# Feeding the last four blocks of the down-projection to the seven-product scheme as well

## The chip, the cores and the metric

The kernel runs on one core of a Trainium2 chip. The metric is the device time of one execution in microseconds (us). Before the change it is 2092.22 us, the median of three runs (2092.10 to 2092.37). The engines are TensorE (PE, matmuls; PEld is its weight load), VectorE (DVE), ScalarE (ACT), GpSimd (POOL) and SyncE (SP, which issues most loads).

## What is computed

Two layers of an encoder over 256 tokens of width 2048, in float32. Cut to the part that the change touches, one layer ends with

```python
h2 = rms_norm(x, ln2_g[l])
u = depthwise_conv(h2 @ w_up[l], conv_w[l], conv_b[l])
gate, up = u[..., :D_FF], u[..., D_FF:]        # D_FF = 5632
x = x + (jax.nn.silu(gate) * up) @ w_down[l]   # (256, 5632) @ (5632, 2048)
```

and the next layer begins with `rms_norm(x, ln1_g) @ w_in`. Ahead of this part stand the two attention groups and the output projection; they are not changed.

## The kernel before, in words

**Precision.** A float32 product is made of three float32r products: each operand is split into a high part (ACT, L112) and a low part (DVE, L113), and high x high, low x high and high x low are added in PSUM. So a product of one 128x128 block of activations with 128x512 weights is three matmuls.

**Weights as a stream.** All weights come in quanta of 128x2048 float32 (1 MB), listed in `quanta` in the order of use (L699 to L729). SP loads a quantum (L741) into one of three `raw` buffers. Each quantum is worked off in steps of 1024 weight columns (two steps; three for a quantum of kind "seven"). Four steps before a step is used, `split_w` (L752) makes its `whi` and `wlo`; there are five buffers of each, and the splits have a raised priority. When the last step of a quantum is split, the load of the quantum three further on is issued.

**The middle and the chunks.** The 5632 middle columns are 44 blocks of 128. `q_up` computes a block (64 pairs of matmuls, two quanta), `glu` (L541) does the conv, the SiLU and the product and leaves the middle `gs[f]`, split, in a tile "mid". The down-projection is done in chunks of 8, 8, 8, 8 and 12 blocks (`CHUNKS`). Output columns 0 to 1023 (nb 0 and 1) of 8 blocks are done pairwise: for a pair of blocks, the 2x2 product over (token halves) x (column halves) takes seven products in place of eight. Six are in `q_seven` (L584): three steps of two products, 18 matmuls 128x512 for a pair; the seventh products of four pairs stand together in a quantum of kind plain (`q_plain`, L639), 12 matmuls, in PSUM tile "mm". `split_seven` (L743) combines the weights on DVE (L747 to L749) ahead of the second step; `sums_mid` (L570) makes the sums and differences of the middles and splits them (L574 to L577 and L580). The six accumulators of a chunk's pairs, `cur["seven"]`, hold one double bank "mm" (of two), both banks "S", and "tr" and "pv": all but one double bank of PSUM. After the chunk's last pair `add_seven` (L611 to L625) adds them to the residual `x`.

Output columns 1024 to 2047 (nb 2 and 3) go through `q_down` (L657): a quantum is four blocks by 512 columns, 24 matmuls in a double bank "mm".

**The last chunk** has 12 blocks. Its first eight go through the plain quantum and four pairs, with the last three `up` blocks between the pairs. Then come, in the order written out at L728, eight quanta of `q_down`: nb 2 for all 12 blocks (three quanta), nb 0 for the last four blocks, nb 3 and nb 1 mixed. The nb 0 and nb 1 quanta accumulate in "mm" and in "tr" and "pv". The last quantum of layer 2 accumulates in the two "S" banks (L679).

**The seam between the layers.** When a column group of `x` is complete, `leave_x` (L627) registers work at a later step: in layer 1 the squares (`square_x`, ACT L140) and the transposes for the next layer (`turn_x`, PE L149, into "S"), whose results `prep_x` splits into the tiles xs0 to xs15 (ACT L115, DVE L116); in layer 2 the output stores. The next layer's first w_in quanta need xs0 to xs3, then xs4 to xs7, and so on.

**What sets the order.** Within an engine the instructions run in an order that is fixed when the kernel is built: by the order of the program, in which work inside `tc.high_priority(offset=...)` counts as that much earlier, and by when buffers come free. So an instruction may be placed behind work that the program lists later. Splits and `add_seven` have an offset of 40 instructions; `add_x` of nb 2, and the plain quantum's add to `x` (L654), have none.

**Tiles for the middles.** `middle` (L518) hands out 17 tiles "mid"; in the last chunk it takes further ones from attention tiles that are idle then (`SPARE`: three "qT").

Of the kernel before, what the change touches and what calls it, by code (L numbers as in the profile page):

```python
# [18 lines left out]
P = 128  # L19
L = 2  # L20
# [32 lines left out]
UP_AT = 56  # L53
WARM = 14

SPARE = 3 * (("qT", 3),)


@with_exitstack
def encoder_kernel(  # L60
# [71 lines left out]
        split(xs[k][:, 0], xs[k][:, 1], src, ln_g[:, which, l, k:k + 1])  # L132

    def square_x(nb):
        if nb == 0:

            st["ss"] = act.tile([P, TT, NB + 24], F32, name="ss_x")[:, :, 0:NB]
        for tt in range(TT):
            sq = work.tile([P, TT, T], F32, name="prob", bufs=2)
            nc.scalar.activation(sq.rearrange("p t n -> p (t n)"), x[:, tt, nb * 512:(nb + 1) * 512], AF.Square,  # L140
                                 accum_out=st["ss"][:, tt, nb:nb + 1])
# [10 lines left out]

    def stat_x(which):
        v = work.tile([P, TT], F32, name="ssum", bufs=2)
        nc.vector.reduce_sum(v, st["ss"], axis=AX.X)
        st["r1"] = act.tile([P, TT], F32, name="r1")
        rsqrt(v, 1.0 / D, st["r1"], "c2")
        if which == 1:

            d = work.tile([P, 4, HD], F32, name="tq", bufs=2)  # L160
            for tt in range(TT):
                nc.vector.tensor_scalar(d[:, tt], ident, st["r1"][:, tt:tt + 1], None, op0=ALU.mult)
            ps = psum.tile([P, T], F32, name="pv", bufs=1)
            mm(ps, ones, d[:, 0:TT].rearrange("p t d -> p (t d)"), True, True)
            st["r2"] = act.tile([P, T], F32, name="acc_b")
            nc.scalar.activation(st["r2"], ps, AF.Copy)
# [351 lines left out]
    def middle(l, f):  # L518

        name, bufs = "mid", MIDS  # L520
        if f >= NF - CHUNKS[-1]:
            k = count[l] = count.get(l, 0) + 1
            if k > MIDS:
                name, bufs = SPARE[k - MIDS - 1]
        return act.tile([P, 2, T], F32R, name=name, bufs=bufs)

    def q_up(l, f, u):
# [13 lines left out]
    def glu(l, f, ps):  # L541
# [20 lines left out]
        gs[f] = middle(l, f)  # L562
        split(gs[f][:, 0], gs[f][:, 1], m)
        ms[f] = m
        if f % 2 and f < NF - CHUNKS[-1] + PART:
            sums_mid(l, f // 2, ms.pop(f - 1), ms.pop(f))

    ms, ss = {}, {}
# [15 lines left out]
    def q_seven(l, c, i):  # L584

        f = sum(CHUNKS[:c]) + 2 * i
        p = f // 2
        a, b = slice(0, P), slice(P, T)

        def body(q, part, hi, lo):  # L590
            if i == 0 and part == 0:
                t = psum.tile([P, 2, 512], F32, name="mm", bufs=2)
                ps = {1: t[:, 0], 6: t[:, 1]}
                for n, name, k in ((5, "S", 2), (7, "S", 2), (3, "tr", 1), (4, "pv", 1)):
                    ps[n] = psum.tile([P, 512], F32, name=name, bufs=k)
                cur["seven"] = ps
            ps = cur["seven"]
            hv, lv = (w.rearrange("p (k n) -> p k n", k=2) for w in (hi, lo))
            todo = (((3, ss[p, 3]), (1, gs[f][:, :, a])),
                    ((7, ss[p, 2]), (5, ss[p, 0])),  # L600
                    ((4, gs[f + 1][:, :, b]), (6, ss[p, 1])))[part]
            for j, (n, x2) in enumerate(todo):
                for x_part, w in ((0, hv), (1, hv), (0, lv)):
                    mm(ps[n], x2[:, x_part], w[:, j], i == 0 and x_part == 0 and w is hv,
                       i == PAIRS - 1 and w is lv)
            if i == PAIRS - 1 and part == 2:
                with tc.high_priority(offset=AHEAD_PRIO):
                    add_seven(ps)
        return body

    def add_seven(ps):  # L611
# [24 lines left out]
            for tt in range(TT):  # L636
                nc.sync.dma_start(out=out[:, tt, m], in_=x[:, tt, m])

    def q_plain(l, c):  # L639

        f0 = sum(CHUNKS[:c])

        def body(q, half, hi, lo):
            if half == 0:
                cur["dn"] = psum.tile([P, TT, 512], F32, name="mm", bufs=2)
            ps = cur["dn"][:, 0]
            hv, lv = (w.rearrange("p (k n) -> p k n", k=2) for w in (hi, lo))
            for x_part, w in ((0, hv), (1, hv), (0, lv)):
                for i in range(2):
                    mm(ps, gs[f0 + 4 * half + 2 * i + 1][:, x_part, 0:P], w[:, i],  # L650
                       half == 0 and i == 0 and x_part == 0 and w is hv, half == 1 and i == 1 and w is lv)
            if half == 1:
                xv = x[:, 0, 0:512]
                nc.vector.tensor_add(xv, xv, ps)  # L654
        return body

    def q_down(l, c, nb, g):  # L657
        f0, nf, i0 = sum(CHUNKS[:c]), CHUNKS[c], FG * g

        def body(q, half, hi, lo):  # L660
            if nb >= 2:
                if nf > PART and i0 == 0 and half == 0:
                    cur["dn"] = psum.tile([P, TT, 512], F32, name="mm", bufs=2)
                ps = cur["dn"]
            elif half == 0:

                ps = cur["dn", nb] = (psum.tile([P, TT, 512], F32, name="mm", bufs=2) if nb == 0 else
                                      _Both(*(psum.tile([P, 512], F32, name=n, bufs=1) for n in ("tr", "pv"))))
            else:
                ps = cur["dn", nb]  # L670
            hv, lv = (w.rearrange("p (k n) -> p k n", k=2) for w in (hi, lo))
            i = i0 + 2 * half

            last = l == L - 1 and c == len(CHUNKS) - 1 and nb == NB - 1
            cut = nf - FG if last or nb < 2 else 0
            if last and i >= cut:
                if i == cut:
                    add_x(nb, ps)
# [14 lines left out]
            with tc.high_priority(offset=4 * AHEAD_PRIO if c == len(CHUNKS) - 1 and nb == NB - 1 else 0):  # L693
                add_x(nb, ps)
            if c == len(CHUNKS) - 1:
                leave_x(q, l, nb, ((3, 0), (1, 1), (5, 0), (1, 1))[nb])
        return body

    for l in range(L):  # L699
# [8 lines left out]
        for c, nf in enumerate(CHUNKS):  # L708
            up = lambda f: [(a["w_up"][l, f, u], q_up(l, f, u), "up") for u in range(2)]
            down = lambda nb, g: [(a["w_down"][l, sum(CHUNKS[:c]) // FG + g, nb], q_down(l, c, nb, g), "")]  # L710
            seven = lambda i: [(a["w_seven"][l, c, i], q_seven(l, c, i), "seven")]

            end = sum(CHUNKS[:c]) + PART + 1
            while f < end:
                quanta += up(f)
                f += 1
            quanta.append((a["w_plain"][l, c], q_plain(l, c), ""))
            if nf == PART:
                for i in range(PAIRS):
                    quanta += seven(i) + down(2 + i // 2, i % 2)  # L720
            else:

                for i in range(PAIRS):
                    quanta += seven(i)
                    if f < NF:
                        quanta += up(f)
                        f += 1
                for nb, g in ((2, 0), (2, 1), (2, 2), (0, 2), (3, 0), (1, 2), (3, 1), (3, 2)):  # L728
                    quanta += down(nb, g)  # L729


    steps = [(q, h) for q in range(len(quanta)) for h in range(3 if quanta[q][2] == "seven" else 2)]
    raw, hl, left, loads, highs = {}, {}, {}, {}, {}

    def load(q, parts=1):
        if q < len(quanta):
            raw[q] = wp.tile([P, 2048], F32, name="raw", bufs=3)
            left[q] = 3 if quanta[q][2] == "seven" else 2
            m = 2048 // parts
            for j in range(parts):  # L740
                loads[q] = nc.sync.dma_start(out=raw[q][:, j * m:(j + 1) * m], in_=quanta[q][0][:, j * m:(j + 1) * m])  # L741

# [138 lines left out]
def _layout(inputs):  # L881
# [29 lines left out]
    o["w_up"] = c(f["w_up"].reshape(L, 2, 8, P, 2, NF, P).transpose(0, 5, 1, 3, 2, 4, 6)).reshape(  # L911
        L, NF, 2, P, 2048)
    wd = f["w_down"]
    n = NF // PART

    four = wd[:, :n * PART * P, :1024].reshape(L, n, PART // 2, 2, P, 2, 512)
    o["w_seven"] = c(np.stack([four[:, :, :, k, :, m] for k, m in ((1, 0), (1, 1), (0, 1), (0, 0))], 4)).reshape(
        L, n, PART // 2, P, 2048)
    o["w_plain"] = c(four[:, :, :, 1, :, 0].transpose(0, 1, 3, 2, 4)).reshape(L, n, P, 2048)
    o["w_down"] = c(f["w_down"].reshape(L, NF // FG, FG, P, NB, 512).transpose(0, 1, 4, 3, 2, 5)).reshape(  # L920
        L, NF // FG, NB, P, 2048)

# [38 lines left out]
```

## Time and profile before

| | |
|---|---|
| median of three runs | 2092.22 us (2092.10 to 2092.37) |
| the profiled execution | 2092.0 us, span 2090.2 us |
| busy: PE, PEld, DVE, ACT, POOL | 2083.5, 1789.2, 1720.5, 1222.3, 170.3 us |
| granted clock of PE | 1.00 |
| DMA | 408.42 MB, mean 195 GB/s |

The profile is of one execution. Its span goes from the first to the last instruction; the 1.8 us between it and the execution's time lie around it. Matmul records overlap (each lasts longer than the distance to the next), so the distance between matmuls is read from groups. The chain of waits is followed back from the last instruction; an engine that isn't on it can be idle without cost.

### The profile page before, as it was taken

How to read it: one execution, taken by the hardware profiler on the slowest of the kernel's cores; microseconds unless marked ns; L12 is line 12 of the kernel's file. 1: busy time of each engine (PE TensorE's matmuls, PEld its weight loads, DVE VectorE, ACT ScalarE, POOL GpSimd, SP SyncE). 2: the span in 40 equal slices, each digit the busy share in tenths (PEclk: the TensorE clock that was granted, in tenths of full speed). 3: DMA queues.
4: the chain of work that ended last, by engine and by line, in shares of the span. 5: the costliest groups of instructions: out<-in, count | busy, mean ns of one | idle time of the engine just before them, and what ended most of it. 6: DMA issues, size and time to landing. Idle time of an engine off the chain costs nothing.

```text
span 2090.2 us, 29185 instructions
## 1 busy us (share of the span) xinstructions
PE 2083.5 (100%) x10816; PEld 1789.2 (86%) x10816; DVE 1720.5 (82%) x2604; ACT 1222.3 (58%) x1817; POOL 170.3 (8%) x237
## 2 busy tenths in 40 slices
PE   9999999999999999999999999999999999999999
PEld 8888888888888888888888888888888888888887
DVE  7786757898898988989757866678989989899896
ACT  7566556555555556556555665565556555555563
POOL 0011100100101001010000011001001010010100
PEclk9999999999999999999999999999999999999999
DMA  9544555556565564655655444555555655556554
GB/s 350 199 145 164 179 172 174 198 195 211 180 241 182 208 210 167 242 193 211 208 181 181 162 160 166 177 182 189 214 202 170 236 199 204 201 185 234 185 200 161
DMA packets 62144, 408.42 MB, mean 195 GB/s; under 512 B 7344, under 2 KB 9904, under 8 KB 13744
## 3 DMA queue, kind: packets, MB, share of 16 engines
q1 hardware_dynamic: 61280, 405.46, 56.2%
q8 instruction: 85, 1.39, 0.3%
q10 hardware_dynamic: 720, 1.08, 0.2%
q14 instruction: 59, 0.48, 0.1%
HBM read 404.42 MB, written 2.10 MB: 194 GB/s over the span
## 4 chain that ended last, share of the span: by engine, by line
PE 99%; DMA 0%; ACT 0%; DVE 0%; issue 0%
PE mm L98 90%; PE S L98 4%; PE pv L98 3%; PE tr L98 2%; PE tr L373 1%; PE tr L307 1%; PE S L149 1%; DMA head<-in_head 0%; ACT qtok L274 0%; ACT kT L315 0%; ACT xs L115 0%; DVE x L688 0%; ACT whi L112 0%
## 5 line engine op out<-in xcount | busy, mean ns | idle before, releaser
L112 ACT ACTIVATE whi<-raw 128x1024 fp32r<-128x1024 f32 (+1 forms) x797 | 830.9, 1057 | 689.9 <-PE mm L98 411.9
L113 DVE TENSOR_TENSOR wlo<-raw,whi 128x1024 fp32r<-128x1024 f32 (+1 forms) x797 | 963.9, 1220 | 270.3 <-ACT whi L112 231.8
L98 PE MATMUL mm<-xs,whi 128*128 128x512 f32 x2816 | 977.0, 390 | 0.0
L98 PE MATMUL mm<-xs,wlo 128*128 128x256 f32 x2816 | 794.1, 282 | 0.0
L98 PEld LDWEIGHTS mm<-xs,whi 128*128 128x128 f32 x2816 | 528.3, 188 | 110.5
L98 PEld LDWEIGHTS mm<-xs,wlo 128*128 128x128 f32 x2816 | 532.2, 189 | 1.1
L98 PE MATMUL mm<-whi,mid 128*128 128x512 f32 x1412 | 368.2, 391 | 0.0
L98 PEld LDWEIGHTS mm<-whi,mid 128*128 128x128 f32 x1412 | 263.0, 188 | 53.9
L98 PE MATMUL mm<-whi,xs 128*128 128x512 f32 x1152 | 294.2, 393 | 1.4 <-ACT qtok L274 1.3
L98 PEld LDWEIGHTS mm<-whi,xs 128*128 128x128 f32 x1152 | 213.1, 188 | 44.7 <-ACT qtok L274 1.8
L98 PE MATMUL mm<-wlo,mid 128*128 128x512 f32 x706 | 202.4, 392 | 0.0
L98 PE MATMUL mm<-wlo,xs 128*128 128x512 f32 x576 | 159.5, 393 | 0.0
L98 PEld LDWEIGHTS mm<-wlo,mid 128*128 128x128 f32 x706 | 132.1, 188 | 27.0
L557 DVE SCALAR_TENSOR_TENSOR pT<-halo,conv,pT 128x256 f32<-128x256 f32 x352 | 148.1, 478 | 0.9
L549 POOL COPY halo<-halo 128x6 f32<-128x6 f32 x88 | 39.6, 450 | 1232.6 <-DVE halo L547 1232.6
L98 PEld LDWEIGHTS mm<-wlo,xs 128*128 128x128 f32 x576 | 107.3, 188 | 21.6
L555 ACT ACTIVATE pT<-halo,conv 128x256 f32<-128x256 f32 x176 | 95.1, 587 | 5.8 <-DVE halo L547 5.7
L550 POOL COPY halo<-halo 128x6 f32<-128x6 f32 x88 | 77.1, 876 | 0.2 <-POOL halo L549 0.2
L547 DVE TENSOR_TENSOR halo<-prob,acc_b 128x512 f32<-128x512 f32 x88 | 60.6, 689 | 1.9
L546 DVE TENSOR_TENSOR prob<-prob,mm 128x512 f32<-128x512 f32 x88 | 59.8, 679 | 0.0
L545 ACT ACTIVATE prob<-mm 128x512 f32<-128x512 f32 x88 | 51.3, 583 | 7.1 <-PE mm L98 7.1
L559 ACT ACTIVATE prob<-pT 128x256 f32<-128x256 f32 x88 | 35.5, 404 | 30.0 <-DVE pT L557 30.0
(180 smaller groups left out, 1475.4 us busy)
## 6 DMA issues: line engine op xcount, KB each, us to landing
raw<-in_w_up SPq DMA_DIRECT2D x176, 1024.0 KB, 4.9
raw<-in_w_in SPq DMA_DIRECT2D x71, 1024.0 KB, 4.9
raw<-in_w_down SPq DMA_DIRECT2D x48, 1024.0 KB, 4.8
raw<-in_w_seven SPq DMA_DIRECT2D x40, 1024.0 KB, 4.9
raw<-in_w_out SPq DMA_DIRECT2D x32, 1024.0 KB, 4.9
raw<-in_w_plain SPq DMA_DIRECT2D x10, 1024.0 KB, 4.8
bias<-in_bias SPq DMA_DIRECT2D x16, 160.0 KB, 3.1
x<-in_x SPq DMA_DIRECT2D x4, 512.0 KB, 10.7
```

Source lines behind the costliest of these rows:

```text
L98: nc.tensor.matmul(ps, lhsT, rhs, start=start, stop=stop, skip_group_check=True)
L112: high = nc.scalar.activation(hi, src, AF.Copy)
L113: nc.vector.tensor_sub(lo, src, hi.bitcast(F32))
L149: nc.tensor.transpose(ps[:, j, tt * P:(tt + 1) * P], x[:, tt, (k + j) * P:(k + j + 1) * P], ident)
L545: nc.scalar.activation(t, ps[:, :, 0], AF.Copy)
L546: nc.vector.tensor_add(t, t, ps[:, :, 1])
L547: nc.vector.tensor_mul(ux[:, :, r:r + T], t, st["r2"][:, None, :].to_broadcast([P, 2, T]))
L549: nc.gpsimd.tensor_copy(ux[:, :, 1:r], ux[:, :, T:T + r - 1])
L550: nc.gpsimd.tensor_copy(ux[:, :, T + r:T + 2 * r - 1], ux[:, :, r + 1:2 * r])
L555: nc.scalar.activation(y[:, j, :], ux[:, j, r:r + T], AF.Identity, scale=w1, bias=b)
L557: nc.vector.scalar_tensor_tensor(y[:, j, :], ux[:, j, o:o + T], w, y[:, j, :], op0=ALU.mult, op1=ALU.add)
L559: nc.scalar.activation(t[:, 0, :], y[:, 0, :], AF.Silu)
```

## The change

The last chunk's four remaining blocks (40 to 43) go through the pair scheme too, for output columns 0 to 1023. Two pairs, and half a quantum of plain products (kind "half": one step, half the load), take the place of the four blocks' nb 0 and nb 1 quanta. The pairs' accumulators stay open until the sixth pair. The order at the chunk's end becomes: nb 2 (three quanta), pair 5, the half plain, pair 6, nb 3 (three quanta). The middles' sums need four more tiles per layer, taken from "kT", "kTb" and "v_a". nb 0 and nb 1 leave (squares and transposes, or stores) after `add_seven`, registered two and three quanta after pair 6; nb 2 is registered two quanta after its last one, at the half plain. The weights on the host are laid out accordingly: w_seven with 22 pairs per layer, w_plain with 6 quanta, the last one half filled. The sums are the same in exact arithmetic.

```diff
-SPARE = 3 * (("qT", 3),)
+STEPS = {"seven": 3, "half": 1}
+
+SPARE = 3 * (("qT", 3),) + 2 * (("kT", 2),) + (("kTb", 1), ("v_a", 1))
...
     def square_x(nb):
-        if nb == 0:
+        if "ss" not in st:
...
-        nc.vector.reduce_sum(v, st["ss"], axis=AX.X)
+        nc.vector.reduce_sum(v, st.pop("ss"), axis=AX.X)
...
+        if name == "v_a":
+            return act.tile([P, 2, 2, T], F32R, name=name, bufs=bufs)[:, 0]
         return act.tile([P, 2, T], F32R, name=name, bufs=bufs)
...
-        if f % 2 and f < NF - CHUNKS[-1] + PART:
+        if f % 2:
             sums_mid(l, f // 2, ms.pop(f - 1), ms.pop(f))
...
+            pairs = CHUNKS[c] // 2
...
-                       i == PAIRS - 1 and w is lv)
-            if i == PAIRS - 1 and part == 2:
+                       i == pairs - 1 and w is lv)
+            if i == pairs - 1 and part == 2:
                 with tc.high_priority(offset=AHEAD_PRIO):
                     add_seven(ps)
+                if c == len(CHUNKS) - 1:
+                    for nb in range(2):
+                        leave_x(q, l, nb, ((2, 0), (3, 0))[nb])
...
-    def q_plain(l, c):
+    def q_plain(l, c, g=0):
-        f0 = sum(CHUNKS[:c])
+        f0 = sum(CHUNKS[:c]) + PART * g
+        steps = CHUNKS[c] // 4
         def body(q, half, hi, lo):
-            if half == 0:
+            first, last = half == 0, half == 1 or 2 * g + half == steps - 1
+            if first:
                 cur["dn"] = psum.tile([P, TT, 512], F32, name="mm", bufs=2)
...
-            if half == 1:
+            if last:
                 xv = x[:, 0, 0:512]
                 nc.vector.tensor_add(xv, xv, ps)
...
-                leave_x(q, l, nb, ((3, 0), (1, 1), (5, 0), (1, 1))[nb])
+                leave_x(q, l, nb, ((2, 0), (1, 1))[nb - 2])
...
-                for nb, g in ((2, 0), (2, 1), (2, 2), (0, 2), (3, 0), (1, 2), (3, 1), (3, 2)):
-                    quanta += down(nb, g)
+                quanta += down(2, 0) + down(2, 1) + down(2, 2) + seven(4) + plain(1) + seven(5)
+                quanta += down(3, 0) + down(3, 1) + down(3, 2)
-    steps = [(q, h) for q in range(len(quanta)) for h in range(3 if quanta[q][2] == "seven" else 2)]
+    steps = [(q, h) for q in range(len(quanta)) for h in range(STEPS.get(quanta[q][2], 2))]
...
-            m = 2048 // parts
+            m = (1024 if quanta[q][2] == "half" else 2048) // parts
```

## Rows read from the trace of the kernel before

**Rows 1.** the page's busy times: us, share of the span, instructions of each engine.

```profile
PE 2083.5 (100%) x10816; PEld 1789.2 (86%) x10816; DVE 1720.5 (82%) x2604; ACT 1222.3 (58%) x1817; POOL 170.3 (8%) x237
```

**Rows 2.** the page's chain that ended last, by engine.

```profile
PE 99%; DMA 0%; ACT 0%; DVE 0%; issue 0%
```

**Rows 3.** the chain in time, layer 2's last chunk: start, us, what.

```profile
1996.96 11.33 PE mm L98 x65
...
2042.54 21.99 PE mm L98 x97
...
2068.61 5.44 PE mm L98 x24
```

**Rows 4.** PE in time, first and last matmuls of that chunk.

```profile
1990.22 1.08 PE L98 MATMUL mm<-whi,mid 128*128 128x512 f32 x4
...
2085.67 0.61 PE L98 MATMUL S<-wlo,qT 128*128 128x512 f32 x2
```

**Rows 5.** the chain in order of time at the seam of the layers.

```profile
1034.21 2.72 PE mm L98 x12
1036.93 0.88 PE S L149 x8
1037.81 9.08 PE mm L98 x40
```

**Rows 6.** busy time by engine in stretches: us, then busy us, PE's clock, DMA.

```profile
572.67:582.01 9.34, 9.34 (x43) 7.75 (x42) 9.23 (x10) 5.46 (x7) 0.00 (x0) 1.00 0.54 195
...
1001.00:1018.00 17.00, 17.00 (x77) 14.08 (x76) 16.91 (x23) 9.36 (x13) 2.19 (x2) 1.00 0.76 265
1018.00:1045.00 27.00, 27.00 (x125) 22.46 (x124) 17.37 (x19) 15.05 (x26) 0.00 (x0) 1.00 0.57 195
1045.00:1066.00 21.00, 21.00 (x106) 17.50 (x105) 13.21 (x19) 12.61 (x22) 0.70 (x1) 1.00 0.51 168
...
2059.00:2087.00 28.00, 27.29 (x121) 22.27 (x119) 13.77 (x14) 5.87 (x6) 0.00 (x0) 1.00 0.27 100
```

**Rows 7.** DVE's groups from 1990 to 2040: busy us, mean ns, idle before.

```profile
L747 DVE TENSOR_TENSOR raw<-raw 128x1024 f32<-128x1024 f32 x3 | 3.6, 1215 | 0.0
L749 DVE TENSOR_TENSOR raw<-raw 128x512 f32<-128x512 f32 x4 | 2.7, 684 | 0.0
...
L113 DVE TENSOR_TENSOR mid<-tq,mid 128x256 fp32r<-128x256 f32 x2 | 0.8, 415 | 0.0
L654 DVE TENSOR_TENSOR x<-x,mm 128x512 f32<-128x512 f32 x1 | 0.7, 675 | 0.0
...
L577 DVE TENSOR_TENSOR tq<-bias,tq 128x128 f32<-128x128 f32 x1 | 0.3, 280 | 0.0
```

**Rows 8.** the page's group of ACT's high parts: busy us, mean ns, idle before.

```profile
L112 ACT ACTIVATE whi<-raw 128x1024 fp32r<-128x1024 f32 (+1 forms) x797 | 830.9, 1057 | 689.9 <-PE mm L98 411.9
```

**Rows 9.** DMA issues: count, KB each, median us to landing.

```profile
raw<-in_w_down SPq DMA_DIRECT2D x48, 1024.0 KB, 4.8
raw<-in_w_seven SPq DMA_DIRECT2D x40, 1024.0 KB, 4.9
```

**Rows 10.** DVE in time, a middle chunk and layer 2's end.

```profile
574.75 4.62 DVE L113 TENSOR_TENSOR wlo<-raw,whi 128x1024 fp32r<-128x1024 f32 x4
...
583.20 1.22 DVE L481 TENSOR_TENSOR x<-x,mm 128x1024 f32<-128x1024 f32 x1
...
2042.81 0.69 DVE L617 TENSOR_TENSOR x<-x,mm 128x512 f32<-128x512 f32 x1
...
2054.01 1.21 DVE L622 TENSOR_TENSOR x<-x,S 128x1024 f32<-128x1024 f32 x1
...
2058.88 0.68 DVE L625 TENSOR_TENSOR x<-x,pv 128x512 f32<-128x512 f32 x1
```

**Rows 11.** DVE in order of time at the seam, the first four preps.

```profile
1039.07 0.87 DVE L116 SCALAR_TENSOR_TENSOR xs<-S,head,xs 128x256 fp32r<-128x256 f32 x2
...
1041.91 0.87 DVE L116 SCALAR_TENSOR_TENSOR xs<-S,head,xs 128x256 fp32r<-128x256 f32 x2
```

More of the change, by code (lines that the diff above doesn't have):

```diff
@@ L650, in body @@
                     mm(ps, gs[f0 + 4 * half + 2 * i + 1][:, x_part, 0:P], w[:, i],
-                       half == 0 and i == 0 and x_part == 0 and w is hv, half == 1 and i == 1 and w is lv)
-            if half == 1:
+                       first and i == 0 and x_part == 0 and w is hv, last and i == 1 and w is lv)
+            if last:
                 xv = x[:, 0, 0:512]
@@ L660, in body @@
         def body(q, half, hi, lo):
[L661 to L670, printed above, removed]
+            if nf > PART and i0 == 0 and half == 0:
+                cur["dn"] = psum.tile([P, TT, 512], F32, name="mm", bufs=2)
+            ps = cur["dn"]
             hv, lv = (w.rearrange("p (k n) -> p k n", k=2) for w in (hi, lo))
@@ L674, in body @@
             last = l == L - 1 and c == len(CHUNKS) - 1 and nb == NB - 1
-            cut = nf - FG if last or nb < 2 else 0
+            cut = nf - FG if last else 0
             if last and i >= cut:
@@ L710, in encoder_kernel @@
             down = lambda nb, g: [(a["w_down"][l, sum(CHUNKS[:c]) // FG + g, nb], q_down(l, c, nb, g), "")]
-            seven = lambda i: [(a["w_seven"][l, c, i], q_seven(l, c, i), "seven")]
             end = sum(CHUNKS[:c]) + PART + 1
@@ L716, in encoder_kernel @@
                 f += 1
-            quanta.append((a["w_plain"][l, c], q_plain(l, c), ""))
+            first = sum(CHUNKS[:c]) // 2
+            seven = lambda i: [(a["w_seven"][l, first + i], q_seven(l, c, i), "seven")]
+            plain = lambda g: [(a["w_plain"][l, c + g], q_plain(l, c, g), "half" if g else "")]
+            quanta += plain(0)
             if nf == PART:
@@ L737, in load @@
             raw[q] = wp.tile([P, 2048], F32, name="raw", bufs=3)
-            left[q] = 3 if quanta[q][2] == "seven" else 2
-            m = 2048 // parts
+            left[q] = STEPS.get(quanta[q][2], 2)
+            m = (1024 if quanta[q][2] == "half" else 2048) // parts
             for j in range(parts):
@@ L913, in _layout @@
     wd = f["w_down"]
[L914 to L919, printed above, removed]
+    n = NF // 2
+    four = wd[..., :1024].reshape(L, n, 2, P, 2, 512)
+    o["w_seven"] = c(np.stack([four[:, :, k, :, m] for k, m in ((1, 0), (1, 1), (0, 1), (0, 0))], 3)).reshape(
+        L, n, P, 2048)
+    plain = np.zeros((L, -(-n // 4) * 4, P, 512), np.float32)
+    plain[:, :n] = four[:, :, 1, :, 0]
+    o["w_plain"] = c(plain.reshape(L, -1, 4, P, 512).transpose(0, 1, 3, 2, 4)).reshape(L, -1, P, 2048)
     o["w_down"] = c(f["w_down"].reshape(L, NF // FG, FG, P, NB, 512).transpose(0, 1, 4, 3, 2, 5)).reshape(
```

## The prediction

> **What bounds the kernel now.** I read the page's busy shares first: PE is busy for 2083.5 of 2090.2 us, DVE for 82%, ACT for 58% [rows 1]. The chain that ended last is 99% PE [rows 2], so nothing but matmul time, and idle time of PE, can move the end. Busy matmul records overlap, so I take the price of a matmul from the chain in order of time: a group of 24 matmuls 128x512 takes 5.44 us, 0.2267 us each [rows 3]. The stretch that the change edits is dense. In layer 2, 97 matmuls from 2042.54 on take 21.99 us, again 0.2267 each, and a block of w_up (64 of the 65 in one piece of 11.33 us) takes 11.1 us [rows 3]. From the last chunk's first plain matmul, at 1990.22, there are 12 + 72 + 192 matmuls 128x512 at 0.2267 us and three blocks of w_up, 95.9 us, which gives 2086.1; the last two matmuls begin at 2085.67 and end by 2086.3 [rows 4]. So no hole is in it. The seam between the layers is as dense: twelve matmuls of a down, eight transposes and the next matmuls follow within 0.05 us [rows 5]. The granted clock is 1.00 (the 2.4 GHz level) in every stretch [rows 6].
>
> DVE is the engine to watch. In the middle of a chunk, where a pair of blocks and a w_down quantum alternate, it is busy for 9.23 of 9.34 us while PE never waits [rows 6]: a full DVE is covered as long as its work is spread over the four steps by which splits run ahead. After the last pair it has room: 17.37 of 27 us and 13.21 of 21 us at the seam, 13.77 of 28 us at the end [rows 6].
>
> **Matmuls.** Per layer the change takes away two w_down quanta (columns 0 to 1023, blocks 40 to 43): 2 x 24 = 48 matmuls. It adds two pairs at 18 and half a plain quantum, 6: 42. That is 6 fewer per layer, 12 in all, 12 x 0.2267 = 2.72 us, and all of it is on the path, because PE is the path. The Trainium skill (TensorE: Matmul & The Clock Gate, section Back-to-back issue gap) gives about 131 ns per matmul of 512 columns as the sustained rate of a real kernel; by that the saving would be 1.57 us, an estimate. The trace doesn't agree: 24 matmuls in 5.44 us are 227 ns each.
>
> **DVE and ACT.** A split of 1024 columns costs DVE 1.16 us in a run (4.62 us for four [rows 10]) and ACT 1.06 [rows 8]. A pair has three splits and, before its second part, three combinations of weights, 1.2 + 0.7 + 0.7 = 2.6 us [rows 7]. The sums of a pair's middles are four operations of 0.28 us and two splits of 0.42, 2.0 us on DVE [rows 7]; on ACT two splits, which I take at the same 0.42. Added per layer on DVE: 7 splits (8.1), two sets of combinations (5.2), two sets of sums (4.0), one plain add (0.7): 18.0 us. Removed: 4 splits (4.6), one add of 1024 columns (1.2) and two of 512 (1.4): 7.2. Net 10.8 us at most, since neighbours overlap. From the end of the fourth pair to the seam's end (1001 to 1066) DVE now works 16.91 + 17.37 + 13.21 = 47.5 of 65 us [rows 6]; with 8.8 more (one set of sums falls earlier) it is 56.3 of 63.6 us. So the total fits, and I cost DVE's and ACT's extra work at nothing where it can spread. ACT gains 7 - 4 = 3 splits and four short ones, about 5 us, and is far from full.
>
> **The tight place.** Let T be the end of the three downs of columns 1024 to 1535 (2042.54 + 16.33 = 2058.9 in layer 2 of the trace). From there PE runs pair 5 (T to T+4.1), the half plain (to T+5.4), pair 6 (to T+9.5) and the first of the three downs of columns 1536 to 2047. There are five buffers for split weights, so the split of pair 6's first part can start at T: ready at T+2.2. Its combinations end at T+4.8, the second part's high half comes at T+5.9 and its low half at T+7.0. PE needs the high half at T+6.8, and the low half four matmuls later, T+7.7. The third part is ready at T+8.2 and its low half is needed at T+9.1; the first half of the next down is ready at T+9.3 and its low half is needed at T+11.3. It holds with 0.7 to 0.9 us to spare: no stall from splits, but the lead is used up here.
>
> **Loads.** Two w_down loads of 1 MB go, two w_seven loads of 1 MB and one of half that come, 0.5 MB more per layer. A 1 MB load lands in 4.8 to 4.9 us [rows 9], and the next down's load goes out when pair 5 is split, about T-2, so it is there at T+3, before its buffers are free. SP carries nothing else here but output stores and, at the seam, two small bias loads. Cost nothing; if that cover went, a late load would cost up to its 4.9 us.
>
> **Waits that the change adds.** The accumulators of the pairs (one double bank "mm", both "S", "tr", "pv") are now held until after pair 6, some 26 us longer. Queued behind that: the additions of the pairs' sums (they were drained between 2042.81 and 2059.56, 16.7 us from the first to the end of the last, sharing DVE with the block's conv and the splits [rows 10]); then, in layer 1, the squares and transposes for the next layer, which need "S"; in layer 2, the last two halves, which accumulate in "S". The sums themselves are 6.5 us of DVE, six of 0.68 and two of 1.2 [rows 7]. After T+9.5 only splits compete (1.16 in each 2.72 us), so they end at about T+9.5 + 6.5/0.57 = T+20.9, and "S" is free at T+18. Layer 2's last quantum needs "S" at T+20.4: enough. At the seam the transposes of columns 1024 to 1535, which come first in the order, take "S" at T+18; four preps took from 1036.93 to 1042.78 [rows 5, 11], 5.9 us, so the transposes of columns 0 to 511 start at T+23.9, and their first prep ends 2.6 us after, as there (1039.07 + 0.48), at T+26.5. w_in's first matmul is due at T+25.9. The lower end is the seam of before, with no wait; the upper end is rival 2. I take the 0.6 us that this gives, once.
>
> **Sum.** The profiled execution took 2092.0 us (span 2090.2); 2092.0 - 2.72 + 0.6 = 2089.9. The median of the runs is 0.2 above it: 2090.1 us.
>
> **Rivals.**
> 1. A bank that isn't free (slower than before). The half plain accumulates in the second "mm" bank; the first belongs to the pairs. The down behind pair 6 needs that bank, so it waits for the plain's add on DVE, due at T+5.4. That add has no raised priority and the splits have. If DVE takes it at once, nothing is lost. If it stands behind the splits of pair 6 and of the next downs (four to six splits, to T+10.5 or T+12.8), the add ends at T+11.2 to T+13.5 and PE stops for 1.7 to 4 us; 2.6 in each layer gives 2092.2 - 2.7 + 5.2 = 2094.7. It decides from 1.36 us per layer on. Against it: adds of this kind got a slot soon after their matmuls (an add of 1024 columns at 583.20, between two splits, on a DVE that was full [rows 10]). For it: DVE has its densest 10 us exactly there. The Trainium skill (PSUM — Partial Sum Buffer, section Engine vs sequencer instructions) says that VectorE's queue is strictly first in, first out; by that, whatever place the compiled order gives the add, nothing passes it. No row here shows it directly. Chance 0.17.
> 2. The seam jams. If the sums take the 16.7 us of now instead of 11.4, the first preps come 5.3 us later and w_in stops for up to 5.5 us, and layer 2's last quantum waits some 1.5 us for "S" (L622 starts 11.2 us after the first sum [rows 10]). Half of that, 3.5 us, gives 2093.0; all of it 2096.5. Against: there is no block's conv beside the sums any more. Chance 0.15.
> 3. Everything is covered, no stall at all: 2089.5. It is the lower end of the forecast's own case.
> 4. A gain beyond the matmuls: there is no idle PE to win in the edited stretches, so I give it 0.03.
>
> **How the numbers follow.** The forecast with its edges (stalls of 0 to 2 us, 2089.4 to 2091.6) has 0.65, rival 1 0.17, rival 2 0.15, rival 4 0.03. The range 2089.2 to 2093.4 holds the first, half of the second rival and the milder third of rival 1 (one layer only, 2092.1), some 8 in 10. A measurement of this kernel tells about 0.2%, 4.2 us, from no change: below 2088.0 or above 2096.4. Faster by that would need 1.5 us more than the matmuls removed: 0.03. Slower by that needs stalls of 6.9 us, rivals 1 and 2 at their upper ends together: 0.06. Within: 0.91.
>
> **What would show it.** Chain still 99% PE; groups of 24 matmuls at 5.44 us; pair 6 beginning 5.44 us after pair 5; no hole before the first down behind pair 6 (if there is one, the DVE add of the plain's bank stands at its end: rival 1); no hole before the first w_in matmul of layer 2 (else rival 2). DVE about 1741 us busy, w_down loads 44, w_seven 44, w_plain 12. I am wrong if the time leaves 2089.2 to 2093.4, or if PE shows holes of over 2 us in all.

## The result, and the profile after

The changed kernel takes 2099.97 us (median of five runs, 2099.66 to 2101.36) against 2092.22 us before it: ratio 1.0039 [1.0029, 1.005]. It is 7.8 us slower, where 2090.1 us was forecast with a range up to 2093.4. The profiled execution took 2099.89 us (span 2098.1). One execution of run 4 below was slow (7316 us) and is left out of that run's median.

The page after: busy times, then the chain that ended last by engine (they answer to [rows 1, 2]).

```profile
PE 2084.9 (99%) x10804; PEld 1788.9 (85%) x10804; DVE 1739.8 (83%) x2642; ACT 1229.6 (59%) x1831; POOL 170.2 (8%) x237
...
PE 98%; DVE 1%; ACT 0%; DMA 0%; issue 0%; DVEq 0%
```

The 12 matmuls are gone (10816 to 10804), and DVE and ACT have the work that was foreseen. Yet PE's share fell and DVE stands in the chain with 1%. So PE now stops. The waits of PE say where (us in total, times, longest); the `qtok` and `halfpi` rows stood there before too, 1.3 and 1.1 us.

```profile
PE S L151 <- DVE xs L118: 4.7, 1, 4.7
PE mm L100 <- ACT qtok L276: 1.3, 2, 0.7
PE mm L100 <- DVE prob L550: 1.1, 2, 0.6
```

To place the loss, follow one landmark through both traces: the first products into "S" of a pair. Of the first pair in layer 1's last chunk they begin at 952.43 before and 952.47 after, so all before that is equal. Of the fourth pair, 998.69 and 999.99 (+1.30). Of layer 2's first pair, 1993.63 and 2001.69 (+8.06). Of its fourth, 2039.89 and 2048.99 (+9.10). So the losses are 1.30 us between the pairs of layer 1, 8.06 - 1.30 + 1.36 = 8.1 us at the seam of the layers (1.36 us is the six matmuls saved in between), and 1.04 us between the pairs of layer 2. 1.30 + 8.1 + 1.04 - 2 x 1.36 = 7.7; the spans differ by 7.9.

**Between the pairs.** PE and DVE in order of time, layer 1, in the last w_up blocks (start, us, engine, line, what, count, wait before it):

```profile
987.42 0.50 PE L100 MATMUL mm<-xs,whi 128*128 128x512 f32 x1 [0.63 <-DVE prob L550]
```

```profile
982.20 0.29 DVE L579 TENSOR_TENSOR tq<-tq,bias 128x128 f32<-128x128 f32 x1
982.40 0.42 DVE L115 TENSOR_TENSOR qT<-bias,qT 128x256 fp32r<-128x256 f32 x1
982.74 1.22 DVE L115 TENSOR_TENSOR wlo<-raw,whi 128x1024 fp32r<-128x1024 f32 x1
983.87 0.28 DVE L581 TENSOR_TENSOR tq<-bias,tq 128x128 f32<-128x128 f32 x1
984.08 1.22 DVE L115 TENSOR_TENSOR wlo<-raw,whi 128x1024 fp32r<-128x1024 f32 x1
985.21 0.42 DVE L115 TENSOR_TENSOR qT<-tq,qT 128x256 fp32r<-128x256 f32 x1
985.55 1.22 DVE L115 TENSOR_TENSOR wlo<-raw,whi 128x1024 fp32r<-128x1024 f32 x1
986.68 0.68 DVE L550 TENSOR_TENSOR prob<-prob,mm 128x512 f32<-128x512 f32 x1
```

DVE has no idle time from 982.20 on. The new sums of the fifth pair (L579, L581 and their splits) stand between weight splits, and L550, the add that frees the "mm" bank for the next w_up block, stands behind all of it. PE waits for that bank. About 0.4 of layer 1's 1.30 us are lost earlier, at 971.55, where the chain of waits goes through late weight splits. DVE had little room here, 47.43 us busy of the 50 from 952 to 1002 before the change; but run 5 will show that the order of its work made these holes, not the amount.

**At the seam.** PE in order of time, then DVE:

```profile
1044.95 1.03 PE L151 MATMUL S<-ident,x 128*128 128x128 f32 x8
1050.66 2.06 PE L151 MATMUL S<-ident,x 128*128 128x128 f32 x8 [4.68 <-DVE xs L118]
1052.61 0.79 PE L100 MATMUL mm<-whi,xs 128*128 128x512 f32 x1
1053.65 2.07 PE L100 MATMUL mm<-whi,xs 128*128 128x512 f32 x4 [0.25 <-ACT xs L117]
```

```profile
1026.26 5.76 DVE L115 TENSOR_TENSOR wlo<-raw,whi 128x1024 fp32r<-128x1024 f32 x5
1031.93 0.68 DVE L625 TENSOR_TENSOR x<-x,mm 128x512 f32<-128x512 f32 x1
1033.56 2.36 DVE L115 TENSOR_TENSOR wlo<-raw,whi 128x1024 fp32r<-128x1024 f32 x2 [0.94 <-ACT whi L114]
1035.84 0.68 DVE L627 TENSOR_TENSOR tq<-tq,mm 128x512 f32<-128x512 f32 x1
1036.71 1.23 DVE L115 TENSOR_TENSOR wlo<-raw,whi 128x1024 fp32r<-128x1024 f32 x1 [0.19 <-ACT whi L114]
...
1044.19 1.22 DVE L632 TENSOR_TENSOR x<-x,tq 128x1024 f32<-128x1024 f32 x1
1045.32 1.21 DVE L483 TENSOR_TENSOR x<-x,mm 128x1024 f32<-128x1024 f32 x1
1046.45 1.22 DVE L115 TENSOR_TENSOR wlo<-raw,whi 128x1024 fp32r<-128x1024 f32 x1
1047.59 0.68 DVE L633 TENSOR_TENSOR x<-x,pv 128x512 f32<-128x512 f32 x1
```

`add_seven`'s sums (L625 to L633) need each other's results and alternate with splits; the last ends at 1048.27. From the start of the first to the end of the last they took 16.3 us, and seven splits stand between them. That is nothing new: before the change the same eight sums took 16.7 us (layer 2, 2042.81 to 2059.56), with seven splits among them as well:

```profile
L113 DVE TENSOR_TENSOR wlo<-raw,whi 128x1024 fp32r<-128x1024 f32 x7 | 8.4, 1218 | 0.0
```

Columns 0 to 511 of `x`, which w_in's first products need, are complete only then. PE has run out of w_down products at 1044.95, turns nb 2 and stops; nb 2's preps (L118), which would free the banks for the next transposes, queue on DVE behind the last sum. From the last sum to the transposes at 1050.66 the chain of waits goes through ScalarE, where the squares of the new `x` (L142) stand ahead of a prep:

```profile
1048.30 1.33 ACT prob L142 x4
1049.64 0.37 ACT xs L117
...
1050.03 0.50 DVE xs L118
```

Before the change the first twelve products of a w_down, eight transposes and the next products followed each other without a gap there [rows 5]. The windows of this stretch, with PE's granted clock as the third number from the end (the layout of [rows 6], where it was 1.00):

```profile
1018.00:1045.00 27.00, 27.00 (x121) 22.32 (x120) 25.38 (x27) 16.32 (x21) 0.00 (x0) 1.00 0.75 273
1045.00:1056.00 11.00, 6.08 (x25) 4.32 (x24) 7.19 (x14) 6.77 (x19) 0.69 (x1) 0.70 0.29 95
```

So of the seam's 8.1 us, 4.92 us is idle PE (11.00 - 6.08). The rest is mainly the lower clock level (granted 0.50 from 1051 to 1055, 1.2 GHz) after the stop: eight transposes take 2.06 us in place of 1.03, four products 2.07 in place of 1.07.

### The profile page after: what moved, and what is told of

Same layout as the page of the kernel before. It is cut to its first block, busy times and chain, and to the rows that moved or that the text cites. A ratio compares the mean times of both kernels' runs of the same rounds, so it can differ in the third digit from the quotient of the medians.

```text
span 2098.1 us, 29235 instructions
## 1 busy us (share of the span) xinstructions
PE 2084.9 (99%) x10804; PEld 1788.9 (85%) x10804; DVE 1739.8 (83%) x2642; ACT 1229.6 (59%) x1831; POOL 170.2 (8%) x237
## 4 chain that ended last, share of the span: by engine, by line
PE 98%; DVE 1%; ACT 0%; DMA 0%; issue 0%; DVEq 0%
PE mm L100 89%; PE S L100 4%; PE pv L100 2%; PE tr L100 1%; PE tr L375 1%; PE tr L309 1%; PE S L151 1%; DVE wlo L115 1%; DMA head<-in_head 0%; DVE prob L550 0%; ACT xs L117 0%; ACT qtok L276 0%; ACT prob L142 0%; ACT prob L549 0%; DVE x L483 0%
## 5 line engine op out<-in xcount | busy, mean ns | idle before, releaser
L550 DVE TENSOR_TENSOR prob<-prob,mm 128x512 f32<-128x512 f32 x88 | 59.9, 681 | 3.4 <-ACT prob L549 3.4
L752 DVE TENSOR_TENSOR raw<-raw 128x1024 f32<-128x1024 f32 x44 | 53.8, 1222 | 0.6
```

Source lines behind the costliest of these rows:

```text
L550: nc.vector.tensor_add(t, t, ps[:, :, 1])
L752: nc.vector.tensor_sub(w[:, 1:3], w[:, 1:3], w[:, 2:4])
```

## The experiments

The theory after reading the traces: the sums at the seam come late because DVE rebuilds the lead of splits that pairs 5 and 6 use up. The rivals: layer 2's part of the change, the order of the transposes, the priority of the sums, the "S" banks, ScalarE's squares. The kernel before ran beside each on the same chip (2092.10 to 2092.28 us).

**1. The change in layer 2 alone** (the old last chunk kept in layer 1).

```diff
...
-            pairs = CHUNKS[c] // 2
+            pairs = CHUNKS[c] // 2 if l == 1 else PAIRS
...
```

> The change in layer 2 alone; layer 1 keeps the old order of its last chunk. My theory (the loss is at the seam of the layers: PE waits 4.7 us for a bank S and then runs some 3 us at the lower clock, about 8 us; beside it each layer loses some 1.1 us in the w_up blocks between the pairs and wins 1.36 us of matmuls): 2092.2 - 1.36 + 1.04 = 2091.9 us, no hole at the seam. Rival (each layer loses alike, half of the 7.7 us): 2096.1 us.

Measured: 2092.58 us, ratio 1.0002 [0.9993, 1.0012]. Without the change at the seam the 7.8 us are gone, which speaks for the theory and against the rival; the saving of 1.36 us does not show. In this trace layer 2's fourth pair begins 0.93 us late, and behind it PE waits another 0.49 us for L550 (to 2044.21): together they use up the saving.

**2. Columns 1024 to 1535 turned last** instead of first.

```diff
-                leave_x(q, l, nb, ((2, 0), (1, 1))[nb - 2])
+                leave_x(q, l, nb, ((6, 1), (1, 1))[nb - 2])
```

> Squares and transposes of columns 1024 to 1535 registered after those of columns 0 to 1023, nothing else; it acts at the seam only. Theory that the order of the S banks makes the hole (columns 1024 to 1535 take both banks first, and w_in's first block waits for their four preps): the hole goes nearly, 2094 us or less. Theory that the sums of the pairs are late (the last addition to columns 0 to 511 ends 3 us after PE has run out of downs, so no order helps before that): the hole shrinks from 8 to about 5 us, 2097 us.

Measured: 2100.87 us, 1.0041 [1.0026, 1.0055]. Both forecasts (2094 or less, 2097) were missed. PE waited in other places, and no shorter, 6.3 us in all (start, us, what, wait; a further wait of 1.76 us for a prep follows):

```profile
1044.45 0.38 PE L151 MATMUL S<-ident,x 128*128 128x128 f32 x2
1047.91 0.88 PE L151 MATMUL S<-ident,x 128*128 128x128 f32 x6 [3.09 <-DVE x L633]
1050.25 0.80 PE L100 MATMUL mm<-whi,xs 128*128 128x512 f32 x1 [1.46 <-ACT xs L117]
```

Two of the eight transposes run, the other six wait for `x` itself, for the last sum (L633). The order of the transposes isn't the cause; the lateness of the sums is enough to stop PE.

**3. A fourfold priority for the sums** (`offset=4 * AHEAD_PRIO` around `add_seven` in the last chunk).

> The additions of the pairs' sums in the last chunk get four times the raised priority, so that they stand ahead of the splits of the next steps. Late-sums theory: they end some 6 us earlier, the seam's hole falls to 0 to 2 us, some 1 us is lost to later splits behind pair 6: 2093 to 2095 us. Order-of-S theory: the transposes of columns 1024 to 1535 still stand at the end of the downs and hold S, so 2098 us or more.

Measured: 2100.17 us, 1.0039. No gain, where the late-sums theory had 2093 to 2095: DVE's order stayed the same, L625 at 1031.61 and L633 at 1047.10. ACT's one step of the sums (L626) stood behind two splits that waited 3.0 us for a w_down load. I read it so (argued, not tested): a priority can't raise a step whose operand isn't there, and in each gap of the chain the next split is ready. Since the order did not change, this run doesn't test what earlier sums would bring.

**4. The sums of the middles registered later** in the last chunk, to clear the w_up stretch.

> The sums of the middles of the last two pairs are registered one pair later, nothing else. Theory that these small DVE operations, put between the splits, upset the order in the w_up blocks (holes of 0.6 us twice per layer): both layers win about 1.1 us back, 2097.7 us with the seam's hole as it is. Rival (the holes come from the split of the weights or the loads there): no change, 2100 us.

Measured: 2100.7 us (four runs), 1.0041. Inconclusive: the built order still took the one operation whose operands are ready early (the difference of the first block's halves) at the same place, at 962.88, and PE's waits for L550's add, one in each layer, stayed (0.8 us).

**5. That operation made late by its data.** v2 = m1a - m1b is also m2b - v1, and v1 needs the pair's second block; the last two pairs of a layer use that.

```diff
-        nc.vector.tensor_sub(v[:, 2], m1[:, a], m1[:, b])
+        if p < NF // 2 - 2:
+            nc.vector.tensor_sub(v[:, 2], m1[:, a], m1[:, b])
+        else:
+            nc.vector.tensor_sub(v[:, 2], m2[:, b], v[:, 1])
```

> For the last two pairs the third of the four middles' differences is computed from the pair's other sum (the same value but for rounding), so that it can't run before the pair's second block is done; nothing else. Theory (that 0.2 us operation, which DVE took between two weight combinations, flips the order of ACT's queue, so that ACT waits for a w_up block before five splits, and PE loses 0.6 us there in each layer): the first hole of each layer goes, 2098.8 us, and the fourth pair of layer 1 starts some 0.6 us earlier. Rival (the other sums or the loads): no change, 2100 us.

Measured: 2098.59 us (2097.30 to 2099.81), 1.0031 [1.0019, 1.0043]. The waits between the pairs are gone in both layers; the fourth pair of layer 1 begins its products into "S" at 998.74 (998.69 before, 999.99 after). In the changed kernel the early difference (L580) stood between two combinations of weights, and ACT then put its step for a w_up block ahead of five splits and waited for it:

```profile
962.97 0.29 DVE L580 TENSOR_TENSOR tq<-bias 128x128 f32<-128x128 f32 x1
...
967.17 0.60 ACT L549 ACTIVATE prob<-mm 128x512 f32<-128x512 f32 x1 [2.94 <-PE mm L100]
967.67 4.84 ACT L114 ACTIVATE whi<-raw 128x1024 fp32r<-128x1024 f32 x5
```

In run 5 that order is gone. DVE has as many sums to do and is even busier, 48.30 of the 50 us, and PE is busy for all 50:

```profile
952.00:1002.00 50.00, 50.00 (x267) 43.28 (x266) 48.30 (x66) 32.01 (x43) 3.53 (x6) 1.00 0.60 209
```

So the order made the holes between the pairs, and not the amount of work. The stop at the seam remains:

```profile
1049.17 0.63 PE L151 MATMUL S<-ident,x 128*128 128x128 f32 x4 [4.51 <-DVE xs L118]
```

**6 to 8. Pairs 5 and 6 earlier**, so that more w_down products lie behind them: right after the first nb 2 quantum (early_pairs), one quantum later (spread_pairs), and the first of these with the tied sum (early_pairs_tied).

```diff
...
-                quanta += down(2, 0) + down(2, 1) + down(2, 2) + seven(4) + plain(1) + seven(5)
-                quanta += down(3, 0) + down(3, 1) + down(3, 2)
+                quanta += (down(2, 0) + seven(4) + down(2, 1) + seven(5) + down(2, 2) + down(3, 0) + plain(1)
+                           + down(3, 1) + down(3, 2))
```

(These are the lines of early_pairs; spread_pairs puts each pair one quantum later.)

> The same work in another order: pair 5 after the first down of columns 1024 to 1535, pair 6 after the second, the half plain after the first down of columns 1536 to 2047 (in its own bank), columns 0 to 1023 leaving after it. Pair 6 ends 6.8 us earlier and has 5.4 us of other matmuls between it and pair 5. Late-sums theory: the sums end before the last down, the seam's hole of 8 us goes, and 2092.2 - 2.7 + 2.3 (the holes in the w_up blocks stay) = 2091.8 us. Rival (DVE has too much to do in the last chunk, whatever the order): 2096 us or more.

> As the run above, but each pair one down later: pair 6 ends only 1.4 us earlier than in the changed kernel, while 5.4 us of other matmuls lie between the pairs. Theory that the sums are late because pair 6 ends late: the hole at the seam stays at about 5 us, 2097 us. Theory that the sums are late because the two pairs stand side by side and use up the lead of the splits: the hole goes, 2092 us.

> The early order with the tied difference. If both theories hold: 2092.2 - 2.7 + 1.0 = 2090.5 us, faster than both kernels; if the tied difference does nothing, as early_pairs.

Measured: 2099.55 (1.0038), 2098.46 (1.0029) and 2097.94 us (1.0026 [1.0016, 1.0037]). All three missed their theory's time (2091.8, 2092 and 2090.5); only part of the loss came back. In early_pairs the sums end at 1043.5 and not at 1048.3, and yet PE stops: 1.8 us for the bank of the sums (L627, both layers) and 2.2 us for nb 0's preps.

```profile
PE mm L100 <- ACT xs L117: 2.2, 1, 2.2
PE mm L100 <- DVE tq L627: 1.8, 2, 0.9
```

So an earlier end of the sums alone isn't enough; the preps, squares and nb 3's add queue on DVE and ACT behind them.

spread_pairs tested whether the sums are late because the two pairs stand side by side and use up the lead of the splits. It speaks against that: its time is nearer to the other theory's 2097. The sums took 16.5 us from first to last there and 18.5 in early_pairs, against 16.3 in the changed kernel. Moving the pairs does not shorten the chain of sums. In spread_pairs the chain of waits at the seam goes back to a w_down load (1025.45 to 1031.15).

**9. Layer 2 alone, with the tied sum.**

> The new scheme in layer 2 alone (layer 1's last chunk as before the change), and the one sum of the last two pairs that was ready early made out of the pair's late results. Theory of the holes between the w_up blocks: layer2_only measured 2092.58 with the second layer's hole of 1.04 us still in it; that hole goes, the six matmuls fewer stay: 2091.2 to 2091.6, no PE wait in layer 2's last chunk. Rival (the small op's place did not make layer 2's hole, the tied sum helped in layer 1 alone): 2092.6 as layer2_only.

Measured: 2091.31 us (2090.79 to 2092.11, 11 runs), 0.9995 [0.9986, 1.0004], no wait of PE in layer 2's last chunk. The expectation holds: the holes of run 1 (0.93 and 0.49 us) are gone, and the six matmuls of this layer are won in the trace, whose span is 1.2 us below that of before. It is 0.97 us below the kernel before in the medians, which the interval doesn't yet tell from none.

**10. "S" read early.** With the tied sum, products 5 and 7 leave their "S" banks as soon as pair 6's second step is done: `read_s` adds product 5 to `x` and copies product 7 into SBUF on ACT.

```diff
...
+            if c == len(CHUNKS) - 1 and i == pairs - 1 and part == 1:
+                with tc.high_priority(offset=AHEAD_PRIO):
+                    read_s(ps)
...
```

> tied_sum, and in the last chunk products 5 and 7 are read out of the two S banks as soon as pair 6's second part is done (one add, one extra ACT copy), so that nb 2's transposes need not wait for add_seven's later sums. Theory of the late sums: nb 0's x is still finished by the last sum some 13 to 15 us after pair 6's last part, so nb 2 is turned early but the first w_in products, which need nb 0, still start late: stop of 3 to 5 us at the layer seam and the low clock after it, 2096.5 to 2098.5. Rival (the S banks are what holds the seam): the stop goes, with it the low clock: 2098.6 - 4.5 - 0.6 - 2.4 = 2091.1.

Measured: 2098.24 us, 1.0028 [1.0017, 1.0039]. As the late sums have it: nb 2 is turned at 1033.67, 10 us earlier, and nothing is gained, since w_in begins with nb 0:

```profile
1046.67 0.88 PE L151 MATMUL S<-ident,x 128*128 128x128 f32 x6 [1.75 <-DVE x L648]
1048.39 0.50 PE L100 MATMUL mm<-whi,xs 128*128 128x512 f32 x1 [0.85 <-ACT xs L117]
1050.95 2.07 PE L100 MATMUL mm<-whi,xs 128*128 128x512 f32 x4 [2.06 <-ACT xs L117]
```

**11. The same, and layer 2's first w_in job begins with nb 2.** Its sum over the input columns is taken in another order.

```diff
...
-            for u in range(4):
-                quanta.append((a["w_in"][l, j, u], q_win(l, j, u), ""))
+            order = (2, 0, 1, 3) if l > 0 and j == 0 else range(4)
+            for n, u in enumerate(order):
+                quanta.append((a["w_in"][l, j, u], q_win(l, j, u, n == 0), ""))
```

> free_s_tied, and the second layer's first w_in job reads its four weight tiles in the order nb 2, nb 0, nb 1, nb 3, so that TensorE has 24 products (24 x 0.2267 = 5.4 us) of nb 2 while the sums of nb 0 and nb 1 drain. Theory of the late sums: the stop of 4.5 us is filled, the clock stays up, at most 1 us of waits: 2090.8 to 2092.5. Rival (the queues of VectorE and ScalarE, and not the lateness of the two quarters, bound the seam; the lag only moves to nb 0's and nb 3's preps): 2096 to 2098.5.

Measured: 2092.09 us (2091.92 to 2092.54), 0.9999 [0.999, 1.0008]: 6.15 us less than run 10 by the order of four weight tiles. PE in order of time at the seam:

```profile
1033.61 1.03 PE L151 MATMUL S<-ident,x 128*128 128x128 f32 x8
...
1044.47 0.39 PE L100 MATMUL mm<-whi,xs 128*128 128x512 f32 x1
...
1050.20 0.82 PE L151 MATMUL S<-ident,x 128*128 128x128 f32 x6
1052.17 0.50 PE L100 MATMUL mm<-whi,xs 128*128 128x512 f32 x1 [1.16 <-ACT xs L117]
1053.44 1.19 PE L100 MATMUL mm<-whi,xs 128*128 128x512 f32 x4 [0.76 <-ACT xs L117]
```

The 24 products of nb 2 fill 1044.47 to 1050.20, while the sums drain. The stop of 4.5 us is gone, 1.92 us of short waits remain, and the clock stays at 1.00:

```profile
1045.00:1056.00 11.00, 9.08 (x44) 7.08 (x44) 7.43 (x12) 7.33 (x18) 0.70 (x1) 1.00 0.57 192
```

**12. The order without the early reading of "S".**

> tied_sum with only the order of the second layer's first four weight tiles changed (nb 2, nb 0, nb 1, nb 3); the S banks are read where add_seven read them. free_s_uord without its early read. Theory (both are needed): nb 2's transposes wait for the S banks until 1043.6, its preps follow 1.5 to 3 us later on queues that still hold sums and splits, a stop of 2 to 4 us and the low clock: 2094.5 to 2097. Rival (the order alone is the cure): 2092.1, as free_s_uord.

Measured: 2095.82 us, 1.0016 [1.0007, 1.0025]. Both are needed: the order alone gives 2.8 of the 6.5 us, since nb 2's preps come behind the sums too; one wait of 3.3 us for them remains and the low level after it.

**13. Products that do nothing in the stop.** With the tied sum, 18 products ahead of w_in's first, overwritten by it.

> tied_sum with 18 extra products of 128x512 (18 x 0.2267 = 4.1 us) issued ahead of the second layer's first w_in product, into its bank, where the first real product overwrites them: they do nothing but keep TensorE at work. Theory (the seam is set by the sums, and TensorE's fall to its lower level follows its stop): the sums end where they did, the stop shrinks from 4.5 us to under 1 us, the transposes and first products run at the upper level (8 transposes 1.03 us, 4 products 0.91 us): 2096 to 2097. Rival 1 (the lower level comes whether it stops or not): 2098.6. Rival 2 (TensorE is the bound there): 2098.6 + 4.1 = 2102.7.

Measured: 2097.99 us (2096.41 to 2098.68), against 2098.59 without them; the spans are equal, 2096.3. 4.1 us of added matmuls cost nothing, so TensorE isn't the bound at the seam: rival 2 falls. The theory holds in that alone. The edit also moved more than was meant. The added products run ahead of the last w_down products, and not in the stop:

```profile
1039.76 4.01 PE L100 MATMUL mm<-whi,kT 128*128 128x512 f32 x17
```

and the sums end at 1044.17, where they ended at 1046.78 without them. So this run doesn't show what the stop alone costs. What is left of it came as two waits of 0.56 and 1.11 us, and the clock fell all the same, so the 2 us were not won:

```profile
1051.00:1053.00 2.00, 1.07 (x6) 0.76 (x7) 1.69 (x7) 1.37 (x4) 0.65 (x1) 0.96 0.02 8
1053.00:1055.00 2.00, 2.00 (x9) 1.61 (x7) 0.90 (x3) 0.48 (x1) 0.04 (x1) 0.50 0.03 8
```

**14. Run 11 with the squares of nb 0, 1 and 3 behind the preps** on ScalarE (a `tc.issue_after` on the last prep), the mean two weight tiles later.

> free_s_uord, and ScalarE squares nb 0, 1 and 3 for the second layer's first norm only after the preps of nb 0 (nb 1); the mean is taken two weight tiles later. In free_s_uord five squares of 0.62 us and their 0.19 us reads stood on ScalarE from 1047.65 to 1051.67, ahead of nb 0's preps, and TensorE waited 1.16 + 0.76 us for those. Theory (the squares make the wait): about 1 us of the 1.92 goes, the rest is the length of transpose and prep: 2091.0 to 2091.4. Rival (the transposes come too late for that anyway): 2092.1.

Measured: 2091.20 us (2091.08 to 2091.97, 11 runs), 0.9996 [0.9987, 1.0004]. As expected: 0.9 us less than run 11, waits of 0.24 and 1.00 us remain.

**15 to 17. The last sum that nb 0 waits for, moved up**: on run 11 (uord_sub), on run 14 (uord_both), and on run 14 in the last chunks alone (last_sub).

```diff
...
         nc.vector.tensor_add(x11, x11, ps[1])
+        nc.vector.tensor_sub(x21, x21, ps[4])
...
-        nc.vector.tensor_sub(x21, x21, ps[4])
...
```

> free_s_uord, and add_seven subtracts product 4 from x21 right after its first sum, so that the last sum which nb 0 waits for is no longer the ninth, behind nb 3's add and two splits. Theory (nb 0's readiness still holds the seam): nb 0's transposes come a few matmuls earlier and cover part of the squares: 2090.8 to 2091.6. Rival (the squares hold the preps alone): 2092.1.

> uord_squares and uord_sub together. Theory: both waits go and TensorE waits under 0.5 us at the seam: 2092.1 - 1.9 = 2090.2, which is the time of before less 2.72 us for the 12 matmuls and plus the 0.7 us that the seam's mixed order still costs. Rival: a wait remains for a third reason (the low parts on VectorE): 2091 to 2092.

> uord_squares, with the subtraction of product 4 moved to the second place of add_seven in the last chunks alone (the other chunks' sums as they were). Theory (what is left of the seam's waits, 0.24 + 1.00 us, is nb 0's late turn): nb 0's x is finished about 3 us earlier, its transposes can come among nb 2's products, the waits shrink below 0.5 us: 2090.2 to 2090.8. Rival (TensorE's order keeps the six transposes behind nb 2's 24 products, so the waits stay): 2091.2. Rival 2 (a subtraction early in the sums costs splits, as it did in the other chunks): over 2092.

Measured: 2109.50 (1.0085), 2105.50 (1.0066) and 2091.34 us (0.9996 [0.9987, 1.0005]). The first two changed more than was meant: every chunk's `add_seven` has this line, and in the others PE now waited for nb 2's or 3's add and for splits (uord_sub):

```profile
PE mm L100 <- DVE x L483: 7.1, 5, 1.5
PE mm L100 <- ACT whi L114: 5.4, 3, 2.3
```

So both missed their forecast, and their times say nothing of the seam. In uord_both's trace the waits there are 0.24 and 1.00 us, as in run 14. last_sub tests it cleanly: no gain. The six transposes stayed behind nb 2's 24 products, at 1050.23, and the waits are 0.24 and 1.00 us as in run 14 (the first rival).

## Why the prediction was wrong

- **Matmuls** held: 12 fewer, dense where nothing else stops PE; layer 2's share shows in run 9 (-0.97 us in the median, 1.36 foreseen).
- **The tight place** held for PE: from pair 5 to the end of the last w_down, 1018 to 1045, it is busy for 27.00 of 27.00 us. But pair 6's last two products stand behind eight of the next w_down, so the pair ends at 1030.60, 1.8 us later than foreseen.
- **Rival 1** did not come about. The half plain's add started at 1025.65, and no wait stands before the next w_down. In early_pairs, in another order, a wait for the other bank came (0.9 us a layer).
- **The seam: the step that failed** is, in "Waits that the change adds", "After T+9.5 only splits compete (1.16 in each 2.72 us), so they end at about T+9.5 + 6.5/0.57 = T+20.9". With T = 1019.26 (pair 5's first product in layer 1 after) that is 1040.2; they ended at 1048.27, T+29.0, 8.1 us later. The first sum began 3.2 us late, at 1031.93: 1.8 us for pair 6's end and 1.3 us for a run of five splits (1026.26 to 1031.93) ahead of it. The other 4.9 us are the sums' length, 16.3 us and not 11.4. The forecast shared DVE out as if sums and splits ran side by side. In the built order seven splits stand between the eight sums, most sums need an earlier one's result, and one step is on ACT (L626, behind two splits that waited for a load until 1032.46). From T+9.5 to their end DVE had 6.1 us of sums (6.5 foreseen), 11.1 us of splits (4.9 foreseen), 1.1 of nb 3's add and 1.1 idle. Both "S" banks were read at 1043.1, T+23.8 (T+18 foreseen), and w_in's first product came at T+33.4 (T+26.5).
- **The lead.** The forecast said that the lead of splits is used up at pair 6, and not who pays for rebuilding it. Four of the five splits in one run are that price (the first is pair 6's own); the seven between the sums are not, since as many stood there before the change.
- **What is shown and what is argued.** That the late sums stop PE at the seam is shown: with nb 2 turned last (run 2) and with the "S" banks read early (run 10) PE waits for the last sum, and work that needs neither nb 0 nor nb 1 (run 11) ends the stop. Why the sums take 16 us is read from the traces; no run took the splits out from between them.
- **Rival 2** (0.15) was the right mechanism: the sums took 16.3 us (16.7 named). That the lengths agree so well is partly luck: the block's conv did go, as was held against this rival, but nb 3's add and idle time of DVE took its place. Its price, up to 5.5 us, matched the idle PE (4.9), but the 3 us of the lower clock level that follow a stop were in no term, and "all of it" at 2096.5 was left outside the range. Its second half did not come: layer 2's last quantum did not wait for "S".
- **DVE at nothing "where it can spread"** failed between the pairs, which cost 1.30 and 1.04 us. The sum took DVE's total (56.3 of 63.6 us) from the fourth pair on and gave the stretch ahead of it no line. But the total isn't what failed: in run 5 DVE is busier there and PE never waits. One small operation, ready early, changed the order on DVE and ACT.
- **Loads at nothing** looked at the first of the three w_down loads behind the pairs. The last one went out at 1027.50, when pair 6's last part was split, and ACT waited 3.12 us for it. DVE stood idle 0.94 us then; what the seam lost by it was not tested by itself.
- What stays open is the last 1.2 us of waits at the seam and 0.7 us in run 11 (layer 2's first pair at 1994.92, 1.29 later than before, is -1.36 + 1.92 of waits + 0.73); the three kernels that come out ahead (runs 9, 14 and 17) do so by 0.9 to 1.0 us, within their intervals.

## What to carry to other kernels

When work goes from the bound engine to an engine with spare time in total, cost the place where results must be complete, and in the order in which that engine will run them: here 6.1 us of dependent sums, with seven splits between them, took 16.3 us, and a trace of before showed 16.7 for the same sums. A share of spare time doesn't say that, and a full engine need not mean a wait (run 5). If the result is late, give the bound engine something that doesn't need it: here the order of four weight tiles, with the banks freed early, was worth 6.5 us (run 5 to run 11), and priorities, earlier pairs or another order of the transposes at most 1.5. And a change to a helper hits all its callers (runs 15, 16): restrict it to the place under test.

## What the runs showed of the hardware

A stop of PE can cost more than its length. In tied_sum, after the wait of 4.51 us, the granted clock was 0.50 of full speed (1.2 GHz) from 1051 to 1055, while PE was busy for 3.76 of the 4 us, and 0.61 from 1055 to 1057, before it was 1.00 again:

```profile
1051.00:1055.00 4.00, 3.76 (x12) 2.64 (x11) 1.94 (x5) 1.38 (x4) 0.70 (x1) 0.50 0.00 0
1055.00:1057.00 2.00, 2.00 (x7) 1.57 (x7) 0.48 (x1) 1.07 (x2) 0.00 (x0) 0.61 0.04 8
```

In warm_seam it fell after two shorter waits (0.56 us, to 1050.14, and 1.11 us, to 1051.75; then 0.50 from 1053 to 1055). In free_s_uord waits of 1.16 and 0.76 us, after a dense stretch, left it at 1.00. What made the difference between these two is not shown here.
